# Wider products for q and k, and a first load order with held loads and eight products of zeros

## The chip, the cores and the metric

The kernel runs on one core of a Trainium2 chip. The metric is the device time of one execution in microseconds. The profile is of one such execution; its engines are TensorE (PE, with PEld for the loads of its stationary operand), VectorE (DVE), ScalarE (ACT), GpSimd (POOL) and SyncE (SP, which here issues every DMA).

## The reference

A decoder trunk of two layers over x of 256 x 1024 in float32. Each layer is a token mixer and a gated MLP with a causal convolution, each followed by `x <- LayerNorm(alpha * x + f(x))`.

```
# layer 0, mixer
u, v = split(gelu(x @ w_in))                 # 1024 -> 2 x 1024
v = layer_norm(v)
y = (u * (causal(w_s) @ v + b_s)) @ w_out    # 8 groups, chunks of 128 positions
# layer 1, mixer: 16 heads of 64, one block of 256 keys
q, k, v = split(x @ w_qkv); q = q * 64 ** -0.5
y = softmax(q @ k.T + bias_by_distance, causal) @ v @ w_o
# each layer
g, val = split(causal_conv3(x @ w_up))       # 1024 -> 2 x 2816
y = (gelu(g) * val) @ w_down
```

## The kernel before

The order of the work is made ahead of time, when the program is built. Every group of instructions is recorded as an operation with an engine, an estimated duration, what it reads and what it writes. `Plan.emit` then goes through all of them as a list scheduler: at each step the engine that can start earliest takes the ready operation that is due first, and the instructions are written out in the order of the planned starts. TensorE's main operations keep the order in which they were recorded, and operations marked `fill` go between them as soon as the plan holds them to be ready. Each engine's queue, SP's DMA queue among them, then runs strictly in that order. What an instruction really waits for on the chip is not taken from the plan: it follows from the memory that the instruction itself reads and writes.

All products are made from a high and a low part of float32 data (`whi`, `wlo` for weights, `xh`, `xl` for x, all float32r): hi·hi + hi·lo + lo·hi. Each 1 MB chunk of weights is loaded into one of two raw buffers (`raws`), ScalarE copies it into `whi` and VectorE subtracts that into `wlo` (`split`, L338 and L344). A chunk is prepared five chunks ahead (`prep`, `spent`); a raw buffer is free again when both parts are made. The chunks follow in one stream: a_v (4 chunks), a_u (4), a_out (4), f_up0, f_dn0, b_v, b_qk (8), b_o, f_up1, f_dn1.

At the start, the transposed x (`xT`) is loaded in four pieces into a scratch area `ff`, and the first two chunks of a_v in five. A `rank` (the numbers in `FIRST` and `XFIRST`) makes their due times; the scheduler otherwise picks as for any operation. `xT` is laid out by row tile t, then k, so a piece of one k has two runs of 128 columns in each partition. `gmlp` multiplies x with a_v in 16 steps (k, t), each of two halves of 512 columns with three products: first k = 0 to 3 for both row tiles, then k = 4 to 7 for t = 0, then for t = 1. Each half takes hi·hi, then hi·lo of the weights, then lo·hi. Then 8 groups of a_u follow (`cols_times`), with LayerNorm of v and the spatial products between them, and the output projection a_out.

In the second mixer, `moba`, `project(i, j)` makes q (j = 0) or k (j = 1) of head pair i with `cols_times`: for each of 8 k three products of 256 columns into the first half of a bank. ScalarE copies the first 128 columns in float32 (L338), and the high part (128 columns for q, 256 for k); VectorE subtracts the low part from the bank (L348). `scores(i - 1)` is recorded after `project(i, 1)`, then `turn(i - 2)`, and `apply(i - 3)` between the two projections; the last pairs follow inside the output projection. `bring` holds the loaded position bias of three head pairs. The up projection (`conv_up`) uses `cols_apart` instead: for each k one product of 512 columns with both parts of x as moving data and one of 256, and `joined` adds the two halves of the bank.

Of the kernel before, what the change touches and what calls it, by code (L numbers as in the profile page):

```python
# [45 lines left out]
T1_WAITS = (2600, 3300, 4000, 4700)  # L46
REST = 25000, 9000, 25000
AHEAD = 12000


class Buf:
# [25 lines left out]
class Plan:  # L77
# [44 lines left out]
    def emit(self):  # L122
        ops = self.ops
        for o in ops:
            for b in o.bufs:
                for q in b.prev:
                    o.deps.update(x for x in q.ops if x is not o)
            assert all(d.i < o.i for d in o.deps), "a group waits for one recorded after it"

        t = 0.0  # L130
        for o in ops:
            o.due = math.inf
            if o.eng == "pe":
                o.due = t
                t += o.ns
        for o in reversed(ops):
            if o.due == math.inf:
                o.due = t
            for d in o.deps:
                d.due = min(d.due, o.due - self.lag(d, o) - (d.ns + (2000.0 if d.eng == "sp" else 0.0)))  # L140
        for o in ops:
            if o.rank is not None:
                o.due = o.rank - 1e6

        succ, left = {}, {}
        for o in ops:
            left[o] = len(o.deps)
            for d in o.deps:
                succ.setdefault(d, []).append(o)
        engines = ("pe", "act", "dve", "pool", "sp")  # L150
        free = dict.fromkeys(engines, 0.0)
        cand = {e: [] for e in engines}
        bus, table = 0.0, None
        order = []
        bulk = [o for o in ops if o.eng == "pe" and not o.fill]
        nb = 0

        def ready(o):
            return max([0.0] + [d.end + self.lag(d, o) for d in o.deps])

        for o in ops:
            if not left[o]:
                cand[o.eng].append((0.0, o))
        while len(order) < len(ops):
            best = None
            for e in engines:
                c = cand[e]
                if e == "pe":
                    c = [x for x in c if x[1].fill or (nb < len(bulk) and x[1] is bulk[nb])]
                if not c:  # L170
                    continue
                s0 = min(max(free[e], r) for r, _ in c)
                now = [x for x in c if max(free[e], x[0]) <= s0 + 1.0]
                if e == "pe":
                    pick = min(now, key=lambda x: (not x[1].fill, x[1].due))
                else:
                    pick = min(now, key=lambda x: x[1].due)
                    for x in c:
                        s = max(free[e], x[0])
                        if x[1].due < pick[1].due and s0 < s < s0 + pick[1].ns and \  # L180
                                s + x[1].ns <= pick[1].due and x[1].due < s0 + pick[1].ns:
                            pick = x
                s = max(free[e], pick[0])
                if best is None or s < best[0]:
                    best = (s, e, pick)
            s, e, pick = best
            o = pick[1]
            cand[e].remove(pick)
            if o.eng == "pe" and not o.fill:
                nb += 1  # L190
            o.start = s
            if e == "sp":
                bus = max(bus, s + 1100.0) + o.nbytes / 360.0
                free[e] = max(s + 475.0, bus - 1500.0)
                o.end = bus
            else:
                extra = 0.0
                if o.table and o.table != table:
                    extra, table = 1300.0, o.table
                o.end = free[e] = s + o.ns + extra  # L200
            order.append(o)
            for x in succ.get(o, ()):
                left[x] -= 1
                if not left[x]:
                    cand[x.eng].append((ready(x), x))
        order.sort(key=lambda o: (o.start, o.i))
        for o in order:
            o.emit()
# [15 lines left out]
def trunk_kernel(ctx: ExitStack, tc: tile.TileContext, a: dict, out: bass.AP):  # L224
# [154 lines left out]
    chunks = {}  # L379


    FIRST = {0: [(0, 512, 0), (512, 1024, 2), (1024, 2048, 4)], 1: [(0, 1024, 6), (1024, 2048, 7)]}
    XFIRST = ((0, 1, 1), (1, 1, 3), (2, 2, 5), (4, 4, 8))

    def prep(i):
        name, c = stream[i]
        raw = raws.new()
        cuts = FIRST.get(i, [(0, CH, None)])
        for s, e, rank in cuts:
            load(raw.ap[:, s:e], a[name][c, :, s:e], [(raw, range(s // 256, e // 256))], rank=rank)  # L390
        subs = []
        for s in range(2):
            hi, lo = whi.new(), wlo.new()
            pieces = [(0, 512), (512, 1024)] if i in FIRST or i in FINE else [(0, SUB)]
            for b, e in pieces:
                src = raw.ap[:, s * SUB + b:s * SUB + e]
                split((hi, range(b // 256, e // 256), hi.ap[:, b:e]), (lo, range(b // 256, e // 256), lo.ap[:, b:e]),
                      (raw, range((s * SUB + b) // 256, (s * SUB + e) // 256), src))
            subs.append((hi, lo))
        chunks[i] = subs  # L400
# [25 lines left out]
    def xt_view(b):  # L426
        return b.ap

    xh, xl = xt_new()
    xT32 = place("ff", HALF, KT * S)  # L430
    xv32 = xT32.ap.rearrange("p (t k c) -> p t k c", t=NT, k=KT)

    def load_xt(k, n, rank):
        load(xv32[:, :, k:k + n, :], a["xT"][:, :, k:k + n, :], [(xT32, [(t, j) for t in range(NT) for j in range(k, k + n)])],
             rank=rank)
        for t in range(NT):
            parts = [(t, j) for j in range(k, k + n)]
            split((xh, parts, xt_view(xh)[:, t, k:k + n, :]), (xl, parts, xt_view(xl)[:, t, k:k + n, :]),
                  (xT32, parts, xv32[:, t, k:k + n, :]), by="dve" if k == 0 else "act")

    prep(0)
    for k, n, rank in XFIRST:
        load_xt(k, n, rank)
    for i in range(1, CHUNKS):
        prep(i)
    xtok = [Buf(t) for t in xs_]
    QUART = range(4)
# [193 lines left out]
    def gmlp():  # L641
        at = xt_at(xh, xl)
        pieces = [[(o, HALF, bank(True)) for o in (0, HALF)] for _ in range(NT)]
        order = [(k, t) for k in range(4) for t in range(NT)] + [(k, t) for t in range(NT) for k in range(4, KT)]
        v = []
        for k, t in order:
            rows_step(pieces[t], *at(k, t), *sub("a_v", k // 2, k % 2), k == 0, k == KT - 1)
            if t == NT - 1 and k % 2:
                spent("a_v", k // 2)
# [110 lines left out]
    def moba(h, l, scr):  # L760
        n4 = KT * S
        oh, ol = place("rr", 0, n4), place("rr", n4, n4)
        pring = Places("ff", [4 * P, 19 * S, 19 * S + P + S, 19 * S + 2 * (P + S)], P + S)
        qkring = [Places("ff", (j * 2 * P, j * 2 * P + P), P) for j in range(2)]
        qkparts = [[Ring(tiles(f"qk{n}{j}", 2, n, F32R)) for j in range(2)] for n in (P, S)]
        ering = Places("ff", [4 * S + x * (P + S) for x in range(6)], P + S)
        bring = Places("ff", [4 * S + 6 * (P + S) + x * 2 * S for x in range(3)], 2 * S)
        ohv, olv = (b.ap.rearrange("p (k s) -> p k s", k=KT) for b in (oh, ol))
        vb = rowring.new()
        vv = vb.ap.rearrange("p (t d) -> p t d", t=NT)  # L770
# [17 lines left out]

        def project(i, j):
            b, t = bank(), qkring[j].new()  # L790
            cols_times(b, h, l, *sub("b_qk", i, j))

            n, at2, scale = (P, P, DH ** -0.5) if j == 0 else (S, 0, 1.0)
            src, (th, tl) = b.ap[:, at2:at2 + n], (x.new() for x in qkparts[j])
            act(t.ap, b.ap[:, :P], AF.Copy, [b], [t], scale=scale, psum=True)
            act(th.ap, src, AF.Copy, [b], [th], scale=scale, psum=True)
            stt(tl.ap, src, scale, th.ap.bitcast(F32), ALU.mult, ALU.subtract, [b, th], [tl])
            t = (t, th, tl)
            held.setdefault(i, []).append(t)
            if j == 0:  # L800
                biases[i] = bring.new()
                load(biases[i].ap, bass.AP(tensor=scr.ap.tensor, offset=scr.ap.offset + 2 * i * DIST,
                                           ap=[[1, P], [DIST, 2], [1, S]]), [biases[i]], [scr])
            else:
                spent("b_qk", i)

        def scores(i):
# [4 lines left out]
            def both(o, seq):  # L812
                return [(bank2[hh].ap[:, o[0]:o[1]], x.ap[hh * DH:(hh + 1) * DH], y.ap[hh * DH:(hh + 1) * DH],
                         n == 0, n == len(seq) - 1) for n, (x, y) in enumerate(seq) for hh in range(2)]

            mms(both((0, P), [(q0, k0)]) + both((P, P + S), [(qh, kh), (qh, kl), (ql, kh)]),
                [q0, qh, ql, k0, kh, kl], bank2, fill=True)
            held[i] = [softmax(bank2[hh], bias, hh) for hh in range(2)]

# [81 lines left out]
def _layout(i):  # L901
# [10 lines left out]
    def paired(wa, wb):  # L912
# [3 lines left out]
    w_in, qkv = np.asarray(i["a_w_in"])[0], np.asarray(i["b_w_qkv"])[0]  # L916
    g = {
        "x": f(x.reshape(NT, P, D).transpose(1, 0, 2)),
        "xT": f(x.reshape(NT, P, KT, P).transpose(3, 0, 2, 1)),
        "a_v": by_rows(w_in[:, D:]),  # L920
        "a_u": f(tiles(w_in[:, :D]).reshape(4, 2, P, SUB).transpose(0, 2, 1, 3).reshape(4, P, CH)),
        "a_out": by_rows(np.asarray(i["a_w_out"])[0]),
# [45 lines left out]
```

## Time and profile before

| | |
|---|---|
| median of 3 runs | 573.56 us (572.23 to 574.41) |
| the profiled execution's own time | 573.82 us |
| its span, first to last instruction | 572.1 us |
| TensorE busy | 557.8 us (98%), 3226 products |
| VectorE busy | 459.9 us (80%) |
| ScalarE busy | 356.0 us (62%) |
| DMA | 110.93 MB, mean 194 GB/s |

The busy time of TensorE is modelled from pipelined products, so 98% does not say that it runs at its peak. The spacing of products in the timeline is the better measure of what one of them costs.

### The profile page before, as it was taken

The numbers are of one execution on the slowest core, as the hardware profiler recorded it, in microseconds if no ns is written. First come the engines' busy times: TensorE is split into PE (matmuls) and PEld (weight loads), VectorE is DVE, ScalarE is ACT, GpSimd is POOL, SyncE is SP. The second block draws the span as 40 slices with busy tenths as digits, with TensorE's granted clock in tenths as the row PEclk, the third lists the DMA queues.
The fourth block names the chain that finished last, engine by engine and source line by source line (L and its number), as shares of the span: only waits on it lengthen the run. The fifth ranks groups of instructions, "written<-read, shape, count | busy, mean of one in ns | idle before, by whom it ended". The sixth has DMA issues, their size and how long they took to land.

```text
span 572.1 us, 8555 instructions
## 1 busy us (share of the span) xinstructions
PE 557.8 (98%) x3226; PEld 482.7 (84%) x3226; DVE 459.9 (80%) x857; ACT 356.0 (62%) x652; POOL 11.5 (2%) x17
## 2 busy tenths in 40 slices
PE   6999999999999999999999999999999999999994
PEld 4799888888888878888899998788888888888884
DVE  4589989999999998467858767589989999997426
ACT  5474558776677786335569666367867767785300
POOL 0020010000000000001000000000000000000001
PEclk9999999999999999999999999999999999999998
DMA  7887644537554657652666542506456446566302
GB/s 259 307 300 288 257 147 158 211 147 255 187 220 149 221 224 263 227 212 92 221 221 236 207 156 84 222 1 211 158 215 226 183 186 214 196 245 231 144 1 73
DMA packets 20133, 110.93 MB, mean 194 GB/s; under 512 B 2251, under 2 KB 6268, under 8 KB 7676
## 3 DMA queue, kind: packets, MB, share of 16 engines
q1 hardware_dynamic: 20092, 110.39, 52.9%
q8 instruction: 25, 0.41, 0.3%
q14 instruction: 16, 0.13, 0.1%
HBM read 109.31 MB, written 1.07 MB: 193 GB/s over the span
## 4 chain that ended last, share of the span: by engine, by line
PE 91%; DMA 4%; DVE 2%; SPq 1%; ACT 0%; issue 0%; DVEq 0%
PE twos L326 52%; PE bank L326 38%; DMA raw<-in_a_v 2%; DMA raw<-in_a_u 2%; DVE wlo L344 1%; PE bank L332 1%; PE twos L332 1%; SPq L355 1%; ACT whi L338 0%; DVE x L348 0%; DVE ff L348 0%; DVE stat L494 0%; DVEq L964 0%; DVE stat L497 0%; DVE stat L499 0%
## 5 line engine op out<-in xcount | busy, mean ns | idle before, releaser
L344 DVE TENSOR_TENSOR wlo<-raw,whi 128x1024 fp32r<-128x1024 f32 (+1 forms) x212 | 228.9, 1103 | 39.2 <-ACT whi L338 38.6
L338 ACT ACTIVATE whi<-raw 128x1024 fp32r<-128x1024 f32 (+1 forms) x212 | 194.8, 954 | 58.7 <-DMA raw<-in_f_dn 24.5
L326 PE MATMUL twos<-xt,whi 128*128 128x512 f32 x640 | 222.2, 394 | 0.0
L326 PE MATMUL twos<-xt,wlo 128*128 128x256 f32 x640 | 177.3, 277 | 0.0
L326 PEld LDWEIGHTS twos<-xt,whi 128*128 128x128 f32 x640 | 120.0, 188 | 27.7
L326 PE MATMUL bank<-whi,rr 128*128 128x512 f32 x432 | 135.1, 391 | 0.0
L326 PEld LDWEIGHTS twos<-xt,wlo 128*128 128x128 f32 x640 | 120.2, 188 | 0.1
L326 PEld LDWEIGHTS bank<-whi,rr 128*128 128x128 f32 x432 | 81.1, 188 | 17.8 <-issue 1.0
L326 PE MATMUL bank<-wlo,rr 128*128 128x512 f32 x216 | 84.1, 389 | 0.0
L326 PE MATMUL bank<-xt,whi 128*128 128x256 f32 x384 | 71.8, 288 | 0.0
L348 DVE SCALAR_TENSOR_TENSOR ff<-ff,convc 128x254 f32<-128x254 f32 (+1 forms) x160 | 69.7, 478 | 0.5 <-ACT ff L338 0.2
L326 PEld LDWEIGHTS bank<-xt,whi 128*128 128x128 f32 x384 | 59.6, 191 | 2.0 <-issue 1.0
L338 ACT ACTIVATE ff<-twos 128x512 f32<-128x512 f32 (+1 forms) x56 | 31.0, 567 | 46.3 <-PE twos L326 43.9
L326 PE MATMUL bank<-xt,wlo 128*128 128x256 f32 x192 | 54.2, 282 | 0.0
L326 PEld LDWEIGHTS bank<-wlo,rr 128*128 128x128 f32 x216 | 40.6, 188 | 8.2
L338 ACT ACTIVATE ff<-ff,convc 128x256 f32<-128x256 f32 x80 | 45.6, 592 | 1.9 <-DVE ff L344 1.4
L326 PE MATMUL twos<-whi,xt 128*128 128x512 f32 x128 | 42.0, 396 | 0.0
L344 DVE TENSOR_TENSOR ff<-twos,ff 128x512 f32<-128x512 f32 (+1 forms) x48 | 30.9, 645 | 13.2 <-ACT ff L338 12.3
L338 ACT ACTIVATE ff<-bank,lncol 128x128 f32<-128x128 f32 x48 | 18.8, 458 | 30.5 <-PE bank L332 30.5
L326 PEld LDWEIGHTS bank<-xt,wlo 128*128 128x128 f32 x192 | 36.7, 191 | 0.0
L348 DVE SCALAR_TENSOR_TENSOR x<-x,bank 128x512 f32<-128x512 f32 x16 | 11.0, 686 | 27.4 <-PE bank L326 27.4
L326 PEld LDWEIGHTS twos<-whi,xt 128*128 128x128 f32 x128 | 24.1, 188 | 4.7
(70 smaller groups left out, 480.4 us busy)
## 6 DMA issues: line engine op xcount, KB each, us to landing
raw<-in_f_up SPq DMA_DIRECT2D x44, 1024.0 KB, 4.8
raw<-in_f_dn SPq DMA_DIRECT2D x22, 1024.0 KB, 4.8
raw<-in_b_qk SPq DMA_DIRECT2D x8, 1024.0 KB, 4.8
lnrow<-in_lnrow SPq DMA_DIRECT2D x5, 1024.0 KB, 5.8
raw<-in_a_u SPq DMA_DIRECT2D x4, 1024.0 KB, 4.7
raw<-in_a_out SPq DMA_DIRECT2D x4, 1024.0 KB, 5.1
raw<-in_b_v SPq DMA_DIRECT2D x4, 1024.0 KB, 4.8
raw<-in_b_o SPq DMA_DIRECT2D x4, 1024.0 KB, 4.8
```

What stands on the lines that cost most here:

```text
L326: nc.tensor.matmul(o, l, x, start=start, stop=stop)
L332: nc.tensor.transpose(o, x, ident.ap)
L338: plan.op("act", ns, lambda: nc.scalar.activation(o, x, func, **kw), r, w, table=table)
L344: dve(70 + 1.04 * flat(x), lambda: nc.vector.tensor_tensor(o, x, y, op=op), r, w)
L348: lambda: nc.vector.scalar_tensor_tensor(o, x, s, y, op0=op0, op1=op1), r, w)
L355: plan.op("sp", nbytes / 360.0, lambda: nc.sync.dma_start(o, src), r, w, nbytes=nbytes, rank=rank)
```

## The change

Start. Loads that have a rank are issued by SP strictly by it, before any other load. Ranks 5, 7, 9 and 10 have a small DMA ahead of them that copies 64 bytes from a part of an earlier load's buffer into a scratch tile (`hold`); the parts are those of ranks 0, 4, 6 and 7. Chunks 2 and 3 get ranks 9 and 10 and buffers of their own, in `ff` and in the row buffer of the LayerNorm weights, and are split in pieces of 512 columns. `xT` is laid out by k, then all 256 rows, so a piece is one run in each partition. The splits of x take two k at once. VectorE fills 512 columns with zeros, and eight products of them are recorded ahead of all others, into a bank that nobody reads. Step k = 0 of a_v runs for both row tiles together: high weights with the high part of x for both, then with the low part, then the low weights.

q and k. `project` uses `cols_apart`. ScalarE copies (scaled) the second half of the bank, VectorE adds the first half, ScalarE copies the high part and VectorE subtracts the low part, both now from SBUF. The buffers in `ff` move; `bring` has two places instead of three.

```diff
+WARM = 8
 # Plan.emit
+        ranked = sorted((o for o in ops if o.rank is not None), key=lambda o: -o.rank)
+                if e == "sp" and ranked:
+                    c = [x for x in c if x[1] is ranked[-1]]
+            if o.rank is not None:
+                ranked.remove(o)
 # trunk_kernel
-    FIRST = {0: [(0, 512, 0), (512, 1024, 2), (1024, 2048, 4)], 1: [(0, 1024, 6), (1024, 2048, 7)]}
+    FIRST = {0: [(0, 512, 0), (512, 1024, 2), (1024, 2048, 4)], 1: [(0, 1024, 6), (1024, 2048, 7)],
+             2: [(0, 2048, 9)], 3: [(0, 2048, 10)]}
     XFIRST = ((0, 1, 1), (1, 1, 3), (2, 2, 5), (4, 4, 8))
+    EARLY = {2: lambda: place("ff", HALF + KT * S, CH), 3: rowring.new}
+    HOLD = {5: (0, 0), 7: (0, SUB), 9: (1, 0), 10: (1, SUB)}
+    scratch = sb.tile([1, 16 * len(HOLD)], F32, name="scratch")
+    loaded, gates = {}, []
+    def hold(rank):
+        i, at = HOLD[rank]
+        g = Buf(scratch[:, 16 * len(gates):16 * len(gates) + 16])
+        load(g.ap, loaded[i].ap[:1, at:at + 16], [g], [(loaded[i], [at // 256])], nbytes=64, rank=rank - 0.5)
+        gates.append(g)
     def prep(i):
-        raw = raws.new()
+        raw = loaded[i] = EARLY.get(i, raws.new)()
         for s, e, rank in cuts:
-            load(raw.ap[:, s:e], a[name][c, :, s:e], [(raw, range(s // 256, e // 256))], rank=rank)
+            if rank in HOLD:
+                hold(rank)
+            load(raw.ap[:, s:e], a[name][c, :, s:e], [(raw, range(s // 256, e // 256))],
+                 gates[-1:] if i <= CHUNKS else (), rank=rank)
     def load_xt(k, n, rank):
+        if rank in HOLD:
+            hold(rank)
+        load(xT32.ap[:, sl], a["xT"][:, sl], [(xT32, parts)], gates[-1:], rank=rank)
+        for j in range(k, k + n, 2):
...
+            split((xh, parts, hv), (xl, parts, lv), (xT32, parts, xv), by="dve" if k == 0 else "act")
+    zeros, idle = place("rr", 0, HALF), bank()
+    dve(480, lambda: nc.vector.memset(zeros.ap.bitcast(F32), 0.0), (), [zeros])
+    for _ in range(WARM):
+        mms([(idle.ap, zeros.ap[:, :P], zeros.ap, True, True)], [zeros], [idle], fill=True)
 # gmlp
+        def first_step():
+            (hi, lo), x = sub("a_v", 0, 0), [at(0, t) for t in range(NT)]
+            for p in range(2):
+                for part, w in ((0, hi), (1, hi), (0, lo)):
+                    for t in range(NT):
+                        o, n, b = pieces[t][p]
+                        mms([(b.ap, x[t][part], w.ap[:, o:o + n], part == 0 and w is hi, False)],
+                            x[t][2][part:part + 1] + [(w, range(o // 256, (o + n) // 256))], [b])
+            plan.tick()
 # moba
-        pring = Places("ff", [4 * P, 19 * S, 19 * S + P + S, 19 * S + 2 * (P + S)], P + S)
-        qkring = [Places("ff", (j * 2 * P, j * 2 * P + P), P) for j in range(2)]
+        pring = Places("ff", [17 * S + x * (P + S) for x in range(4)], P + S)
+        qkring = [Places("ff", (j * 2 * S, j * 2 * S + S), S) for j in range(2)]
+        sring = Places("ff", [23 * S], S)
-        bring = Places("ff", [4 * S + 6 * (P + S) + x * 2 * S for x in range(3)], 2 * S)
+        bring = Places("ff", [4 * S + 6 * (P + S) + x * 2 * S for x in range(2)], 2 * S)
         def project(i, j):
-            cols_times(b, h, l, *sub("b_qk", i, j))
+            cols_apart(b, 0, h, l, *sub("b_qk", i, j))
-            src, (th, tl) = b.ap[:, at2:at2 + n], (x.new() for x in qkparts[j])
-            act(t.ap, b.ap[:, :P], AF.Copy, [b], [t], scale=scale, psum=True)
-            act(th.ap, src, AF.Copy, [b], [th], scale=scale, psum=True)
-            stt(tl.ap, src, scale, th.ap.bitcast(F32), ALU.mult, ALU.subtract, [b, th], [tl])
+            (th, tl), c = (x.new() for x in qkparts[j]), sring.new()
+            act(c.ap, b.ap[:, S:], AF.Copy, [b], [c], scale=scale, psum=True)
+            stt(t.ap, b.ap[:, :S], scale, c.ap, ALU.mult, ALU.add, [b, c], [t])
+            split((th, [0], th.ap), (tl, [0], tl.ap), (t, [0], t.ap[:, at2:at2 + n]))
 # _layout
-        "xT": f(x.reshape(NT, P, KT, P).transpose(3, 0, 2, 1)),
+        "xT": f(x.reshape(NT, P, KT, P).transpose(3, 2, 0, 1).reshape(P, KT * S)),
```

## Rows read from the trace of the kernel before

**Rows 1.** The page's fourth part: the chain of work that ended last, as shares of the span by engine.
```profile
PE 91%; DMA 4%; DVE 2%; SPq 1%; ACT 0%; issue 0%; DVEq 0%
```

**Rows 2.** Busy time by stretch (us from the span's start): the stretch and its length, then busy us and instructions of PE, PEld, DVE, ACT and POOL, the granted clock of TensorE (1.00 is full), the DMA engines' share and GB/s.
```profile
5.00:15.00 10.00, 9.92 (x30) 7.60 (x31) 6.72 (x14) 5.91 (x13) 0.00 (x0) 1.00 0.95 329
15.00:30.00 15.00, 13.66 (x59) 10.64 (x58) 6.78 (x8) 7.46 (x10) 0.00 (x0) 1.00 0.84 312
30.00:60.00 30.00, 29.77 (x238) 28.89 (x237) 29.04 (x48) 18.26 (x30) 3.70 (x3) 1.00 0.82 303
291.00:364.00 73.00, 73.00 (x604) 65.58 (x604) 54.83 (x179) 54.04 (x149) 0.00 (x0) 1.00 0.49 177
```

**Rows 3.** Whom TensorE's products waited for in the whole span: us in total, times, the longest.
```profile
PE bank L326 <- DVE xt L361: 5.0, 1, 5.0
PE bank L326 <- DVE wlo L344: 1.3, 2, 0.8
PE twos L326 <- DVE ff L348: 0.2, 1, 0.2
```

**Rows 4.** Timeline of TensorE in the first stage: start us, busy us, engine, line, operation, the count of merged instructions. The row at 32.11 is the first product with a_u.
```profile
5.00 0.77 PE L326 MATMUL bank<-whi,xt 128*128 128x512 f32 x1 [5.00 <-DVE xt L361]
5.85 0.79 PE L326 MATMUL bank<-wlo,xt 128*128 128x512 f32 x1
...
7.29 0.63 PE L326 MATMUL bank<-wlo,xt 128*128 128x512 f32 x1
...
8.57 0.63 PE L326 MATMUL bank<-wlo,xt 128*128 128x512 f32 x1
...
11.13 0.54 PE L326 MATMUL bank<-wlo,xt 128*128 128x512 f32 x1
...
12.66 0.39 PE L326 MATMUL bank<-wlo,xt 128*128 128x512 f32 x1
...
13.35 0.39 PE L326 MATMUL bank<-wlo,xt 128*128 128x512 f32 x1
...
32.11 0.40 PE L326 MATMUL bank<-xt,whi 128*128 128x256 f32 x2
```

**Rows 5.** Timeline of SP's queue at the start: issue of xT's third piece, of chunk 1 in two pieces, of chunks 2 and 3.
```profile
3.80 0.55 SPq L355 DMA_DIRECT2D ff<-in_xT  x1
4.40 1.07 SPq L355 DMA_DIRECT2D raw<-in_a_v  x2
...
10.93 4.51 SPq L355 DMA_DIRECT2D raw<-in_a_v  x2
```

**Rows 6.** Timeline of ScalarE: its first copy out of each newly landed load, and in brackets the idle time before it and what ended it.
```profile
4.29 0.63 ACT L338 ACTIVATE whi<-raw 128x512 fp32r<-128x512 f32 x1 [2.21 <-DMA raw<-in_a_v]
...
8.94 1.15 ACT L338 ACTIVATE whi<-raw 128x512 fp32r<-128x512 f32 x2 [0.97 <-DMA raw<-in_a_v]
...
11.85 2.42 ACT L338 ACTIVATE whi<-raw 128x512 fp32r<-128x512 f32 x4 [0.57 <-DMA raw<-in_a_v]
...
17.84 2.01 ACT L338 ACTIVATE whi<-raw 128x1024 fp32r<-128x1024 f32 x2 [2.27 <-DMA raw<-in_a_v]
21.67 2.01 ACT L338 ACTIVATE whi<-raw 128x1024 fp32r<-128x1024 f32 x2 [1.83 <-DMA raw<-in_a_v]
...
29.00 2.01 ACT L338 ACTIVATE whi<-raw 128x1024 fp32r<-128x1024 f32 x2 [2.21 <-DMA raw<-in_a_u]
```

**Rows 7.** DMA issues of the whole span: destination and source, count, KB of each, median us from issue to landing.
```profile
out<-x SPq DMA_DIRECT2D x8, 128.0 KB, 1.9
raw<-in_a_v SPq DMA_DIRECT2D x2, 256.0 KB, 3.5
...
lncol<-in_lncol SPq DMA_DIRECT2D x1, 24.0 KB, 6.4
```

**Rows 8.** Timeline of TensorE: two rows of the q and k stage, seven steps of three products apart, and two of the first up projection, eight steps of two products apart.
```profile
322.98 0.40 PE L326 MATMUL bank<-xt,whi 128*128 128x256 f32 x2
...
325.49 0.40 PE L326 MATMUL bank<-xt,whi 128*128 128x256 f32 x2
...
141.92 0.39 PE L326 MATMUL twos<-xt,whi 128*128 128x512 f32 x1
...
144.69 0.39 PE L326 MATMUL twos<-xt,whi 128*128 128x512 f32 x1
```

**Rows 9.** Timeline at the end of the q and k stage: the last pair's high and low part of k, its scores, and the low part of its attention output.
```profile
353.43 0.38 ACT L338 ACTIVATE qk<-bank 128x256 fp32r<-128x256 f32 x1 [0.56 <-PE bank L326]
...
354.01 0.42 DVE L348 SCALAR_TENSOR_TENSOR qk<-bank,qk 128x256 fp32r<-128x256 f32 x1
...
355.55 0.61 PE L326 MATMUL twos<-qk,qk 64*128 64x256 f32 x6
...
364.22 0.42 DVE L344 TENSOR_TENSOR rr<-twos,rr 128x256 fp32r<-128x256 f32 x1
```

**Rows 10.** The position bias: the last maximum of pair 0 on VectorE and the bias load issued behind it (timeline), a line of the chain by time that holds pair 2's scores (start us, us, count), and the bias loads of the whole span with their median landing.
```profile
301.37 0.29 DVE L827 CUSTOM_DVE_ANT_0 ff<-twos,ff 128x128 f32<-128x128 f32 x1
...
301.69 0.38 SPq L355 DMA_DIRECT2D ff<-rbscr  x1
...
313.45 0.78 PE twos L326 x10
...
ff<-rbscr SPq DMA_DIRECT2D x8, 256.0 KB, 4.3
```

More of the change, by code (lines that the diff above doesn't have):

```diff
@@ L430, in trunk_kernel, with cut @@
     xT32 = place("ff", HALF, KT * S)
-    xv32 = xT32.ap.rearrange("p (t k c) -> p t k c", t=NT, k=KT)
     def load_xt(k, n, rank):
[L434 to L439, printed above, removed]
-    prep(0)
-    for k, n, rank in XFIRST:
-        load_xt(k, n, rank)
-    for i in range(1, CHUNKS):
+        def cut(j, m):
+            return slice(j * S, (j + m) * S), [(t, i) for t in range(NT) for i in range(j, j + m)]
+        sl, parts = cut(k, n)
+        if rank in HOLD:
+            hold(rank)
+        load(xT32.ap[:, sl], a["xT"][:, sl], [(xT32, parts)], gates[-1:], rank=rank)
+        for j in range(k, k + n, 2):
+            m = min(2, k + n - j)
+            sl, parts = cut(j, m)
+            hv, lv = (both[:, j:j + m, o:o + S] for o in (0, S))
+            xv = xT32.ap[:, sl].rearrange("p (k x) -> p k x", k=m)
+            split((xh, parts, hv), (xl, parts, lv), (xT32, parts, xv), by="dve" if k == 0 else "act")
[3 more added lines that the diff above has]
+        mms([(idle.ap, zeros.ap[:, :P], zeros.ap, True, True)], [zeros], [idle], fill=True)
+    prep(0)
+    for x in XFIRST[:3]:
+        load_xt(*x)
+    prep(1)
+    load_xt(*XFIRST[3])
+    for i in range(2, CHUNKS):
         prep(i)
@@ L645, in gmlp @@
         v = []
+        def first_step():
[7 more added lines that the diff above has]
+            plan.tick()
         for k, t in order:
+            if k == 0:
+                if t == 0:
+                    first_step()
+                continue
             rows_step(pieces[t], *at(k, t), *sub("a_v", k // 2, k % 2), k == 0, k == KT - 1)
@@ L814, in both @@
                          n == 0, n == len(seq) - 1) for n, (x, y) in enumerate(seq) for hh in range(2)]
-            mms(both((0, P), [(q0, k0)]) + both((P, P + S), [(qh, kh), (qh, kl), (ql, kh)]),
+            q0_, k0_ = (type(t)(t.ap[:, :P]) for t in (q0, k0))
+            mms(both((0, P), [(q0_, k0_)]) + both((P, P + S), [(qh, kh), (qh, kl), (ql, kh)]),
                 [q0, qh, ql, k0, kh, kl], bank2, fill=True)
```

## The prediction

> **What bounds the kernel now.** I read the page first. The chain that ended last lies 91% on TensorE [rows 1], so what counts is where TensorE stands still or runs slowly, and how many products it must run. Next I read whom it waits for: over the whole run it lists 5.0 us before the first product, 1.3 us for low halves of weights, and 0.2 us later [rows 3]. From 41 us to the last product it has work without a gap. A microsecond won before 41 us therefore reaches the end, if nothing after it was hidden behind it; so does a microsecond of product time won in the q and k stage, where TensorE is busy for all of its 73 us [rows 2].
>
> The timeline of the first stage shows more than the list of waits. The v projection is 8 x 2 x 2 x 3 = 96 products of 512 columns. At the spacing of 12.66 to 13.35, three products in 0.68 us, they would take 96 x 0.2275 = 21.8 us; from 5.00 to the first a_u product at 32.11 they took 27.1 us [rows 4]. So 5.3 us are lost after the start, in three places:
> - Clock: from 7.29 to 8.57 three products take 1.28 us, 0.427 each, the 1.2 GHz level; from 12.66 on 0.2275, the 2.4 GHz level [rows 4]. The column of the granted clock reads 1.00 in these stretches [rows 2], so I go by spacing. Thirteen products start before 11.13: 13 x (0.427 - 0.2275) = 2.6 us.
> - Order: those thirteen took 6.13 us, not 13 x 0.427 = 5.55. The second product needs the low half of the first weights, and waits from 5.43 to 5.85: 0.6 us in all.
> - Data: the other 83 took 32.11 - 11.13 = 20.98 us, not 18.9: 2.1 us, at the third and fourth weight chunks.
>
> The data comes late because there are two raw buffers: chunk 2 is issued at 10.93, chunk 3 some 4 us later [rows 5]; ScalarE gets them at 17.84 and 21.67, and the first a_u chunk at 29.00 [rows 6].
>
> **Parts, start.** *Products of zeros.* The memset, some 0.2 to 0.7 us on an idle VectorE, lets them begin near 1.6. Eight at 0.427 us end at 5.0, just when the first data is there; at worst they push it by 0.1. Before, the clock rose 6.1 us after the first product (5.00 to 11.13); the busy stretch now begins 3.4 us earlier, so I put the rise at 7.8. Bounds: risen by 5.0, or at 11.1 as before. At 7.8, 6.5 products run at the low level instead of 13: **-1.3 us** (bounds -2.6 and 0).
>
> *Order of step k = 0.* Both row tiles take the high half before any takes the low half, so four to six products hide the 0.7 us of the split: **-0.6 us** (bounds 0 and -0.6).
>
> *Loads.* The 64-byte loads write a scratch that nothing reads, while each reads a buffer that an earlier load fills. So SP stops at it until that earlier load has landed, and what is issued next need not wait for the 64 bytes themselves. Behind the stopped load stands all of SP's queue. Gate by gate: the first waits for part 0, which is there at 4.29 [rows 6], and SP is free for it near 3.8, where xT's third piece is issued now [rows 5]: half a microsecond. The second waits for the last part of chunk 0, there at 8.9 before [rows 6]; with x in runs twice as long I take 8.2. The first half of chunk 1 is queued by then, so the DMA engines still have 768 KB. The second half of chunk 1 is then issued near 8.8 and lands near 12.3 (a load of 256 KB took 3.5 us from issue to landing [rows 7]). The gate of chunk 2 opens when the first half of chunk 1 is there (11.85 before [rows 6], 11.0 now): issued at 11.5, landed behind 1 MB of others at 16. The gate of chunk 3 opens at 12.3; it lands at 18.6. Against 17.84 and 21.67 that is 2 and 3 us sooner, since these two now have memory of their own, and a_u's first chunk, next in the first raw buffer, follows near 21 instead of 29. TensorE, with the rise at 7.8, finishes k = 0 at 9.1, waits 0.5 for the low half of k = 1 and 0.3 at k = 2, reaches chunk 2 at 17.9 (high half there at 16.6, low at 17.4, now split in pieces of 512) and chunk 3 at 20.6 (19.2, 19.9). Of 2.1 us some 0.75 stay: **-1.35 us** (bounds 0 and -2.1).
>
> Start together: **-3.2 us**, the v stage ends near 28.9. Who could give it back? VectorE is busy 29.0 of the 30 us from 30 to 60, but idle for 3.3 us of 5 to 15 and 8.2 us of 15 to 30 [rows 2]: with a_u's first two chunks landing 8 us sooner, their 4.7 us of low halves move into that idle time, more than the 3.2 us by which the stage moves up.
>
> The Trainium skill, "DMA: Bandwidth & Descriptors", section "Anatomy of one DMA", says that DMA engines do not wait on semaphores, the issuing sequencer does, and that a small transfer still costs about 2 us; by it a chain of four gates, if each had to land, would add some 8 us of DMA silence (an estimate from that page). The shortest landing here, 1.9 us for a store, agrees with the second half, and a 24 KB load behind large ones took 6.4 [rows 7].
>
> **Parts, q and k.** Each of 16 halves has 8 steps of three 256-column products, now one of 512 and one of 256: the columns are the same, 128 products fewer. From 322.98 to 325.49 seven steps of three take 2.51 us, 0.359 each; the up projection already has the pair, and eight take 2.77 us, 0.346 [rows 8]. 128 x 0.013 = **-1.7 us** (1.4 to 2.0 by the rounding of these rows; 0 in a rival below). The Trainium skill, "TensorE: Matmul & The Clock Gate", section "Back-to-back issue gap", gives a product about 2.5 ns beyond its columns; by that the saving would be 0.3 us. The rows give 13 ns, and I go by them.
>
> The price: evacuation is now copy, add, copy, subtract, four steps over two engines, instead of copy and subtract. VectorE gets about 16 x 0.42 = 6.7 us more [rows 9], on 54.8 of 73 us; ScalarE less than that on 54.0 [rows 2]: hidden. What is late next is scores, by about two operations, 0.8 us. Within the stage the next projection covers it. At the end there is less cover: the last pair's low half ends at 364.6 [rows 9], and by the count of products in the output projection it is wanted near 365.3. I take 0 and bound it by 1 us. The bias ring of two instead of three makes load i wait for the maximum of pair i - 2: the third buffer's successor went out at 301.69, right behind the maximum of pair 0 [rows 10]; pair 2's load would go there now, it lands some 4.3 us later, and its scores run at 313.45 [rows 10]: hidden. The rest of the layout change moves buffers only: 0, hidden by the same projections; 1 us at most if one of them is wanted early.
>
> **Sum.** -1.3 - 0.6 - 1.35 - 1.7 = -4.9 us. Against the profiled execution's own 573.82 (span 572.1 and 1.7 around it) that is **568.9**; the median before, 573.56, lies 0.3 lower. 0.5% is 2.9 us, about what a measurement of this kernel tells from no change; faster means below 570.7.
>
> **Rivals.**
> - *The gates hold the loads too long* (the other side: slower). If every held load leaves only after the 64 bytes landed behind all that is queued, each gate drains the queue and then costs about 2 us in which nothing moves (1.9 us for the shortest landing, 6.4 for a small one in the queue [rows 7]). Chunk 1's second half then lands near 16, chunk 2 near 22, chunk 3 near 26.7, and the v stage ends near 36.5: 4.4 us later than now, with q and k still -1.7: 576.5. It decides from chunk 3 landing later than about 23. For it: the plan itself counts such a wait. Against it: no other instruction takes the scratch as an operand. 0.10.
> - *The clock does not rise earlier*, zeros or not: the 1.3 us go, and a slower first stage waits less for data: the v stage ends near 30.5, -1.6 - 1.7: 570.5. For it: nothing here ran zeros. 0.13.
> - *The start is given back* on VectorE between 30 and 60, where it has 1 us of idle time [rows 2]: only q and k remain, about 572.1. For it: 97% busy; against it: 11 us of idle time before. 0.12.
> - *q and k save nothing*, because a product costs only its columns or because scores come late at the end: -3.2: 570.6. Against it: the measured pair [rows 8]. 0.07.
> - The forecast, 0.58, with its own range 567.0 to 570.4.
>
> Faster takes the forecast and about half of the second and fourth cases, on the edge of the bound: 0.70. Within 0.5%: the third, the other halves: 0.21. Slower: the first, 0.09. The range for 8 in 10 runs from the clock risen by 5.0 and data that keep up (about 2 us under the forecast) to just beyond the start given back: 566.8 to 572.5.
>
> **What would show it.** Eight products before 5.0, and the spacing of 0.2275 from about 7.8; no gap after the first real product; chunk 2 with ScalarE near 16, chunk 3 near 18.6, a_u's first chunk near 21; the first a_u product near 28.9; TensorE without waits from there to the end; the q and k steps at 0.346, the stage about 1.7 us shorter. The prediction is wrong if SP stands at a gate while the DMA engines are silent, if the spacing stays at 0.427 until 11, if TensorE waits for VectorE between 30 and 60, or if scores or the last pair hold it after 350.

## The result: slower, and the profile after

The changed kernel takes 577.97 us (median of 6 runs, 575.26 to 579.66) against 573.49 for the kernel before: ratio 1.0088, 95% interval [1.0067, 1.0109]. The forecast was 568.9. The profiled execution took 576.64, its span is 574.9 (572.1 before).

The list of whom TensorE waited for, whole span (us in total, times, the longest), answers to [rows 3]:

```profile
PE bank L338 <- ACT ff L344: 2.1, 4, 0.6
PE bank L332 <- DVE nhalf L445: 1.5, 1, 1.5
PE bank L332 <- ACT whi L344: 0.9, 1, 0.9
PE twos L332 <- ACT xt L344: 0.9, 1, 0.9
PE bank L332 <- DVE wlo L350: 0.4, 2, 0.2
```

Before, all that counted was in the first 41 us. Now there are five waits for ScalarE, 3.0 us together, at tiles of the LayerNorm's way back into columns (`ff`, `xt`). The chain that ended last shows ScalarE too, 2% where [rows 1] have 0%:

```profile
PE 91%; DMA 5%; ACT 2%; DVE 1%; issue 1%; SPq 0%; DVEq 0%
```

Where the 2.8 us between the two profiled executions lie, from the starts of TensorE's products at the edges of each stretch (in the up projections and at the end of q and k, those with the low weights):

| stretch | before | after | change |
|---|---|---|---|
| start to first a_u product | 32.11 | 30.04 | -2.07 |
| to the up projection, first layer (with the first passage through LayerNorm) | 62.78 | 64.01 | +1.23 |
| first up projection, its 320 steps | 111.05 | 113.15 | +2.10 |
| to the products of q and k (second passage) | 84.77 | 86.00 | +1.23 |
| q and k | 62.34 | 61.36 | -0.98 |
| to the second up projection (third passage) | 40.02 | 41.50 | +1.48 |
| to the last product, and from it to the end of the span | 179.03 | 178.84 | -0.2 |

The start and the q and k stage won 3.05 us. Three passages lost 3.94, and the first up projection, of which the diff touches nothing, lost 2.10.

Start, TensorE's timeline, against [rows 4] (zeros, first real products, the wait at the third chunk, the first a_u product):

```profile
1.51 3.78 PE L332 MATMUL bank<-rr 128*128 128x512 f32 x8 [1.51 <-DVE nhalf L445]
5.09 1.68 PE L332 MATMUL bank<-whi,xt 128*128 128x512 f32 x4
6.61 0.62 PE L332 MATMUL bank<-wlo,xt 128*128 128x512 f32 x2
7.07 1.17 PE L332 MATMUL bank<-whi,xt 128*128 128x512 f32 x4
...
18.49 0.51 PE L332 MATMUL bank<-whi,xt 128*128 128x512 f32 x1 [0.92 <-ACT whi L344]
...
30.04 0.40 PE L332 MATMUL bank<-xt,whi 128*128 128x256 f32 x2
```

Four products take 1.52 us from 5.09, the next two 0.46: the spacing falls from the 1.2 GHz level to 0.23, the 2.4 GHz level, shortly after 6 us. Before, that was at 11.

ScalarE's first copies from chunk 1 in its two parts, from chunks 2 and 3 and from the first a_u chunk, against [rows 6]; and SP's queue around the gates, against [rows 5]:

```profile
10.21 1.16 ACT L344 ACTIVATE whi<-raw 128x512 fp32r<-128x512 f32 x2 [0.60 <-DMA raw<-in_a_v]
12.93 1.16 ACT L344 ACTIVATE whi<-raw 128x512 fp32r<-128x512 f32 x2 [1.56 <-DMA raw<-in_a_v]
...
17.81 2.19 ACT L344 ACTIVATE whi<-ff 128x512 fp32r<-128x512 f32 x4 [2.50 <-DMA ff<-in_a_v]
20.28 2.20 ACT L344 ACTIVATE whi<-lnrow 128x512 fp32r<-128x512 f32 x4 [0.28 <-DMA lnrow<-in_a_v]
22.97 1.06 ACT L344 ACTIVATE whi<-raw 128x1024 fp32r<-128x1024 f32 x1 [0.49 <-DMA raw<-in_a_u]
```
```profile
10.27 0.51 SPq L361 DMA_DIRECT2D scratch<-raw  x1
10.82 0.58 SPq L361 DMA_DIRECT2D ff<-in_a_v  x1
12.92 0.50 SPq L361 DMA_DIRECT2D scratch<-raw  x1
13.47 0.58 SPq L361 DMA_DIRECT2D lnrow<-in_a_v  x1
```

A gate is issued once the part that it reads has landed, and the load behind it 0.55 us later; nobody waits for the 64 bytes. Chunk 2 is with ScalarE as late as before (17.81, 17.84), chunk 3 1.4 us and a_u's first chunk 6 us sooner.

The first passage, TensorE's timeline, first of before, then of after:

```profile
85.77 0.60 PE L332 MATMUL bank<-ident,x 128*128 128x128 f32 x4
86.12 0.48 PE L326 MATMUL twos<-whi,xt 128*128 128x512 f32 x1
86.44 0.39 PE L326 MATMUL twos<-wlo,xt 128*128 128x512 f32 x1
86.67 0.40 PE L326 MATMUL twos<-whi,xt 128*128 128x512 f32 x1
86.91 0.60 PE L332 MATMUL bank<-ident,x 128*128 128x128 f32 x4
```
```profile
85.55 1.04 PE L338 MATMUL bank<-ident,x 128*128 128x128 f32 x8
87.10 0.44 PE L338 MATMUL bank<-ident,ff 128*128 128x128 f32 x2 [0.51 <-ACT ff L344]
88.10 0.44 PE L338 MATMUL bank<-ident,ff 128*128 128x128 f32 x2 [0.57 <-ACT ff L344]
88.29 0.48 PE L332 MATMUL twos<-whi,xt 128*128 128x512 f32 x1
```

Before, transposes and products of the up projection take turns, and ScalarE works behind the products. After, twelve transposes stand in a row, and TensorE waits for ScalarE twice. The diff edits none of these instructions; their written order has changed. The same pair of waits is back near 389 us, and one of 0.89 at 278.

The first up projection, eight steps apart, against 141.92 and 144.69 of [rows 8] (2.77 us):

```profile
150.07 0.40 PE L332 MATMUL twos<-xt,whi 128*128 128x512 f32 x1
...
152.90 0.40 PE L332 MATMUL twos<-xt,whi 128*128 128x512 f32 x1
```

Now 2.83 us. By the full resolution of the starts a pair takes 0.3533 us where it took 0.3467, evenly over the whole stage; the second up projection runs at 0.3467 in both.

### The profile page after: what moved, and what is told of

The parts are those of the page before. It is cut to its first block, busy times and chain, and to the rows that moved or that the text cites. A ratio compares the mean times of both kernels' runs of the same rounds, so it can differ in the third digit from the quotient of the medians.

```text
span 574.9 us, 8307 instructions
## 1 busy us (share of the span) xinstructions
PE 561.4 (98%) x3106; PEld 477.7 (83%) x3106; DVE 464.2 (81%) x874; ACT 361.0 (63%) x654; POOL 10.2 (2%) x17
## 4 chain that ended last, share of the span: by engine, by line
PE 91%; DMA 5%; ACT 2%; DVE 1%; issue 1%; SPq 0%; DVEq 0%
PE twos L332 52%; PE bank L332 37%; DMA raw<-in_a_u 3%; DMA raw<-in_a_v 2%; PE twos L338 1%; PE bank L338 1%; ACT ff L344 1%; ACT whi L344 1%; DVE wlo L350 1%; DVE x L354 0%; SPq L361 0%; ACT ff L803 0%; ACT xt L344 0%; DVE ff L354 0%; DVE stat L532 0%
## 5 line engine op out<-in xcount | busy, mean ns | idle before, releaser
L350 DVE TENSOR_TENSOR wlo<-raw,whi 128x1024 fp32r<-128x1024 f32 (+1 forms) x208 | 224.7, 1096 | 41.9 <-ACT whi L344 41.7
L344 ACT ACTIVATE whi<-raw 128x1024 fp32r<-128x1024 f32 (+1 forms) x208 | 191.6, 957 | 58.5 <-PE bank L332 31.4
L332 PE MATMUL twos<-xt,wlo 128*128 128x256 f32 x640 | 179.5, 280 | 0.0
L332 PE MATMUL bank<-xt,whi 128*128 128x256 f32 (+1 forms) x256 | 71.0, 347 | 0.0
L354 DVE SCALAR_TENSOR_TENSOR ff<-ff,convc 128x254 f32<-128x254 f32 (+1 forms) x160 | 67.4, 478 | 1.2 <-ACT ff L344 1.2
L344 ACT ACTIVATE ff<-ff,convc 128x256 f32<-128x256 f32 x80 | 44.0, 594 | 14.5 <-DVE ff L350 14.4
L332 PEld LDWEIGHTS bank<-xt,whi 128*128 128x128 f32 x256 | 44.0, 190 | 6.8 <-issue 1.0
L332 PE MATMUL twos<-whi,xt 128*128 128x512 f32 x128 | 40.8, 392 | 0.9 <-ACT xt L344 0.9
```

The source lines that it names most:

```text
L332: nc.tensor.matmul(o, l, x, start=start, stop=stop)
L344: plan.op("act", ns, lambda: nc.scalar.activation(o, x, func, **kw), r, w, table=table)
L350: dve(70 + 1.04 * flat(x), lambda: nc.vector.tensor_tensor(o, x, y, op=op), r, w)
L354: lambda: nc.vector.scalar_tensor_tensor(o, x, s, y, op0=op0, op1=op1), r, w)
```

## The experiments

Two questions: who makes the waits in the passages, and what makes the pair slower. The first has an offline clue. Going through the written plan of each kernel, one finds stretches in which the plan itself leaves TensorE idle:

```
planned TensorE idle after 30 us (us from start: us idle)
before, only q and k      none
after, only the start     87: 0.78  88: 0.77  88.5: 0.37 | 264: 0.10 0.10  266: 1.40 | 375: 0.78  376: 0.77
```

In the plan a gate is a load that must land before the next one is issued, about 2 us for each; four gates move the planned start by 8 us. The list scheduler then meets all later choices at other times.

### One part of the change at a time, and the gates

`a_start` has all hunks of the start and leaves `project` of q and k as before; `a_qk` has the hunks of `moba` alone. In `a_unplanned` the gates stay in SP's queue, but the loads behind them don't name them, so the plan counts no wait:

```diff
-                 gates[-1:] if i <= CHUNKS else (), rank=rank)
+                 (), rank=rank)
...
-        load(xT32.ap[:, sl], a["xT"][:, sl], [(xT32, parts)], gates[-1:], rank=rank)
+        load(xT32.ap[:, sl], a["xT"][:, sl], [(xT32, parts)], rank=rank)
```

`a_nohold` has no gates: `HOLD = {}`.

> Only the start of the change; q and k as before. Theory 1 (the planner): the gates count in the plan as loads that must land, the plan therefore runs up to 12 us behind the chip at the start, and its order at the three passages from a LayerNorm to the next projection leaves TensorE waiting there, 1.1, 1.2 and 1.4 us in the profile of the changed kernel. Then the v stage ends near 30.0, 2.1 us sooner than before, the three waits stand as in the changed kernel, and the time is 573.5 - 2.1 + 3.7 = 575.1 (up to 2.1 more if the steps of an up projection take 0.353 instead of 0.347 again). Rival (q and k): the passages are disturbed by the new q and k evacuation. Then the waits are not here and the time is about 571.4.

> Only the change of q and k; the start as before. Theory 1: the plan up to the q and k stage is that of the kernel before, so none of the three waits, and the stage alone counts: steps at 0.346 give 573.5 - 1.7 = 571.8, steps at 0.353, as seen in the changed kernel, 573.5 - 0.8 = 572.7. Rival (q and k cost): the longer evacuation or the smaller bias ring makes TensorE wait for scores: at or above 573.5, with waits between 291 and 364 us.

> The changed kernel, whose plan no longer lets the loads wait for the gates (they take no gate among what they read); the gates still stand in SP's queue at the same ranks, so the chip waits at the same places. Theory 1: the plan is closer to the chip, the waits at the first and the third passage go, one of about 0.9 us stays at the second, and the time is 573.5 - 2.1 - 1.0 + 1.0 = 571.4 (up to 2.1 more with slow steps in an up projection, 0.8 less with fast ones in q and k). Rival (the chip): an earlier start leaves VectorE and ScalarE with a backlog at the first passage whatever the order is; then the waits stay at 3.7 us and the time at 575 or more.

> The changed kernel without the four gates; the strict order of the ranks, the buffers of their own for chunks 2 and 3, the zeros and the q and k part stay. Theory 1: as without the gates in the plan, 571.4 and no wait at the first and third passage. What the gates do on the chip: if they keep large loads from taking the bandwidth of small ones, the first half of chunk 0 and the pieces of x come later here and TensorE waits more before 10 us; if the queue runs in order anyway, chunk 2 is with ScalarE at 17.8 or sooner and the v stage ends at 30.0 or sooner.

Measured, beside 572.15 us for the kernel before on the same chip:

| run | us | ratio, 95% interval | first a_u product | pair in the two up projections |
|---|---|---|---|---|
| a_start | 577.76 | 1.0096 [1.0065, 1.0126] | 31.31 | 0.3533, 0.3467 |
| a_qk | 571.55 | 0.9995 [0.9979, 1.0012] | as before | 0.3467, 0.3467 |
| a_unplanned | 571.50 | 0.9987 [0.9970, 1.0005] | 31.69 | 0.3467, 0.3467 |
| a_nohold | 570.18 | 0.9962 [0.9943, 0.9981] | 28.84 | 0.3467, 0.3467 |

The start alone makes the loss. In its list of waits the passages stand as in the changed kernel; with the same gates in the queue but out of the plan they are gone, but for 0.3 us in the second:

```profile
PE bank L338 <- ACT ff L344: 2.1, 4, 0.6
...
PE twos L332 <- ACT xt L344: 0.9, 1, 0.9
```
```profile
PE bank L332 <- ACT whi L344: 2.0, 1, 2.0
PE bank L332 <- DVE nhalf L445: 1.5, 1, 1.5
PE bank L332 <- DVE wlo L350: 0.7, 3, 0.2
PE twos L332 <- DVE xt L350: 0.3, 1, 0.3
```

(The first fence is of `a_start`, the second of `a_unplanned`.) On the chip gates are no gain either: without them the three late chunks are with ScalarE at 16.22, 18.70 and 21.20 (17.81, 20.28, 22.97 with them), and the first a_u product is the earliest of all. Over all profiled executions, chunk 2 is with ScalarE at 16.2 to 17.5 in the three kernels without gates (`b_ten` and `b_cold`, below, are the others) and at 17.8 to 19.5 in the four executions with all four; the first a_u product comes at 28.8 to 30.4 and at 30.0 to 31.7, which overlap. `a_nohold` beats both kernels.

### The planner alone

`c_late` is the kernel before with one number of the planner changed, and no instruction more or less:

```diff
-        bus, table = 0.0, None
+        bus, table = 8000.0, None
```

> The kernel before, with not one instruction added or taken away: only the planner is told that the load bus is taken until 8 us, as if the first loads landed that much later, so that its list of instructions comes out in another order. The plan then holds the same waits of TensorE as that of the changed kernel: 0.78, 0.77 and 0.43 us in the first passage, 1.40 in the second, 0.78 and 0.77 in the third. Theory 1 (the planner's order alone makes the passages' waits): TensorE waits for ScalarE near 87, 277 and 390 us, 3.7 us together, the first product with a_u near 32.1 as before, 572.5 + 3.7 = 576.2 us, and 2.1 us more for each up projection that falls into the slower spacing: 576 to 580. Theory 2 (the gates or the other loads on the chip make the waits, the plan only mirrors them): no wait in the passages, 572.5 us.

Measured: 578.83 us beside 572.24 for the kernel before, ratio 1.0106 [1.0083, 1.0129], first a_u product at 31.96. Its list of waits (the first line is the wait for the first data, as in [rows 3]):

```profile
PE bank L326 <- DVE xt L361: 5.0, 1, 5.0
PE bank L332 <- ACT ff L338: 2.2, 4, 0.6
PE bank L326 <- DVE wlo L344: 1.5, 2, 0.8
PE twos L326 <- ACT xt L338: 0.9, 1, 0.9
...
```

The same five waits for ScalarE stand at the same places, and both up projections run at 0.3533. No gate, no zeros, no new load order, no wider product: the written order alone costs as much as the whole change did. That settles the passages. All traces agree with it: from the last product of the first mixer's output projection to the first of the 320 steps TensorE takes 13.87 to 13.89 us in the four profiled executions with these waits (the changed kernel twice, `a_start`, `c_late`) and 12.45 in the eight others, and the third passage takes 41.4 to 41.5 us against 39.9 to 40.1. Which of the scheduler's choices tips over is not settled; by the plan, one or two gates leave the passages without idle time, three give 2.4 us, four 5.1.

### Two gates, and the zeros

`b_two` keeps the gates ahead of the third and fourth chunk: `HOLD = {9: (1, 0), 10: (1, SUB)}`. `b_ten` and `b_cold` have no gates and `WARM = 10` and `WARM = 0`; both have plans without idle time in the passages.

> The changed kernel with two of its four gates, those ahead of the third and the fourth chunk of a_v. The plan holds no wait in the three passages with two gates (four give 5.0 us, three 2.4 us). Theory 1 (the passages' waits come from the planner, which counts a gate's landing as waited for): no TensorE wait over 0.2 us in the passages near 87, 277 and 389 us, and the first up projection at 0.3467 us for a pair of products; the start pays for two gates on the chip: a_u between 28.84 (none) and 31.69 (four, unplanned), say 30.0, and a total of 570.2 - 0.4 + 1.2 = 571.0 us. Rival A (any gate in the plan brings the passages' waits): about 574. Rival B (gates help where they stand ahead of half megabytes, by leaving the queues to the small loads): a_u at 28.8 or before, 569.8 or less.

> The changed kernel without any gate, and with ten products of zeros instead of eight. Without gates the plan still holds one wait of 0.85 us of TensorE in the passage before the products of q and k, and the run without gates (570.18 us) shows 0.38 us there; with ten products of zeros the plan comes out without that wait. Theory 1 (a wait that the plan holds is paid on the chip, and nothing else differs): 570.2 - 0.4 = 569.8 us, no idle stretch of TensorE between 250 and 290 us, the first product with a_u still at 28.8. Rival (the passage is paid elsewhere, as the softmaxes set the pace of the stage of q and k): 570.2, with the products of q and k starting earlier and the second up projection not. If the pair of products in the first up projection falls into its slower spacing (0.3533 instead of 0.3467 us), 2.1 us come on top of either.

> The changed kernel without any gate and without the eight products of zeros; order and place of the first loads as there. Theory 1 (the zeros are worth what the prediction said, 1.3 us, since the clock then rises behind real products): first product with a_u at 30.1 instead of 28.84; the plan has no wait in the passages here, which gives back 0.4: 570.2 + 1.3 - 0.4 = 571.1 us. Rival (the loads and their splitting set the start, and the zeros only fill a wait): a_u at 28.9, 569.8 us. In between: the first chunks' products are slower but the wait for the third chunk takes part of it, about 0.5 us left.

Measured, beside 572.62 us:

| run | us | ratio, 95% interval | first a_u product | pair in the two up projections |
|---|---|---|---|---|
| b_two | 576.57 | 1.0058 [1.0038, 1.0079] | 31.27 | 0.3533, 0.3533 |
| b_ten | 570.85 | 0.9975 [0.9962, 0.9988] | 30.39 | 0.3467, 0.3467 |
| b_cold | 570.67 | 0.9963 [0.9948, 0.9978] | 29.86 | 0.3467, 0.3467 |

`b_two` is as the first theory has it in the passages: no wait (its one wait behind 30 us is 0.9 us, at 39). The rest of that theory fails: the time is 5.6 us above its 571.0, and both its up projections run at the slow spacing, twice 2.1 us. Eight steps of the first take 2.83 us:

```profile
149.67 0.40 PE L332 MATMUL twos<-xt,whi 128*128 128x512 f32 x1
...
152.50 0.40 PE L332 MATMUL twos<-xt,whi 128*128 128x512 f32 x1
```

So the slow spacing does not need the passages' waits, and it is worth as much as they are.

`b_cold` shows what the zeros are worth. Its clock rises behind real products, late:

```profile
5.04 2.23 PE L332 MATMUL bank<-whi,xt 128*128 128x512 f32 x4 [5.04 <-ACT whi L344]
...
9.63 1.05 PE L332 MATMUL bank<-wlo,xt 128*128 128x512 f32 x2
10.49 0.63 PE L332 MATMUL bank<-whi,xt 128*128 128x512 f32 x1
...
11.23 0.63 PE L332 MATMUL bank<-whi,xt 128*128 128x512 f32 x2
11.69 0.40 PE L332 MATMUL bank<-wlo,xt 128*128 128x512 f32 x1
```

Two products take 0.86 us up to 10.49, the 1.2 GHz level, and two take 0.46 from 11.23, the 2.4 GHz level. Yet the first a_u product comes at 29.86, between the two runs with zeros (28.84, 30.39), and the time ratio equals that of `a_nohold`. Both figures fall between the two expectations: the first product nearer to the theory that prices the zeros (30.1), the time, by its ratio, nearer to the rival. The zeros are worth no more than what these runs differ by among themselves: the first a_u products of the two runs with zeros lie 1.55 us apart. That difference comes from the loads: ScalarE's copy of chunk 0's last part starts at 8.32 and 10.04 in the two runs with zeros, from the same queue of loads. In `b_cold` TensorE, slower at first, waits for nothing behind its first product; in `a_nohold` it waits 0.6 us in the first stage, in `b_ten` 1.8. `b_ten` was to be 0.4 us faster than `a_nohold` for its plan without idle time; its later start hides that, and the run is inconclusive.

### The two spacings

`b_again` is the changed kernel once more. `c_marks` is `b_two` with the first product of a sum run again ahead of itself, at five places of each up projection:

```diff
+AGAIN = {5: (512,), 8: (256,), 11: (128,), 14: (512, 512), 17: (512, 512, 512)}
...
+            for n in twice:
+                o, l, x = seq[0][:3]
+                nc.tensor.matmul(o[:, :n], l, x[:, :n], start=True, stop=True)
```

> The changed kernel itself once more, for the spacing of its products. Theory 1 (the slower spacing in the first up projection follows from the order of what TensorE does before it): 0.3533 us for a pair of products there again, and 0.3467 in the second, with the time near 577.9. Theory 2 (which of the two spacings a stage falls into differs from execution to execution): the first stage can be at 0.3467, with 575.8, or the second at 0.3533, with 580.

> The kernel with two gates (first and second up projection both at 0.3533 us for a pair of products), in which, at five places of each up projection, the first product of a sum is run again ahead of itself and overwritten: once with 512 columns, once with 256, once with 128, then twice and three times with 512; eight extra products of some 1.4 us in each stage, the order and all else as before. Theory 1 (a spacing is a state that TensorE's stream carries on from product to product, set by the entrance into the stage): an extra product shifts the stream against itself and at one or more of the five places the spacing goes from 0.3533 to 0.3467 us and stays there to the next mark. Theory 2 (the spacing is set by what stands around the stage in this kernel: where its tiles lie, what the other engines do): 0.3533 us between all the marks of the stage.

`b_again`: 576.32 us in its one execution, with the stages exchanged: the first up projection at 0.3467, the second at 0.3533. Eight steps of each:

```profile
149.79 0.39 PE L332 MATMUL twos<-xt,whi 128*128 128x512 f32 x1
...
152.56 0.39 PE L332 MATMUL twos<-xt,whi 128*128 128x512 f32 x1
```
```profile
449.66 0.40 PE L332 MATMUL twos<-xt,whi 128*128 128x512 f32 x1
...
452.49 0.40 PE L332 MATMUL twos<-xt,whi 128*128 128x512 f32 x1
```

2.77 us, then 2.83. The same program in the same order (the two traces list the same 3106 products one after the other): so the order does not fix which spacing a stage gets, and my first theory of this run falls. Whether both executions ran on the same chip is not recorded.

`c_marks`: 578.33 us, also one execution. Around its second mark, eight steps before it, the extra product of 256 columns, eight steps after it:

```profile
125.32 0.40 PE L336 MATMUL twos<-xt,whi 128*128 128x512 f32 x1
...
128.14 0.40 PE L336 MATMUL twos<-xt,whi 128*128 128x512 f32 x1
...
128.50 0.28 PE L334 MATMUL twos<-xt,whi 128*128 128x256 f32 x1
...
128.97 0.39 PE L336 MATMUL twos<-xt,whi 128*128 128x512 f32 x1
...
131.75 0.39 PE L336 MATMUL twos<-xt,whi 128*128 128x512 f32 x1
```

2.82 us before, 2.78 after (0.3533 and 0.3467 by the full resolution). The five marks do: once 512, stays at 0.3533; 256, falls to 0.3467; 128, back to 0.3533; twice 512, 0.3467; three times 512, 0.3533. In the second up projection the five do exactly the same. Each spacing holds until the next mark. So the spacing is a state that TensorE's stream of products carries along, set by what came just ahead; neither the places of tiles nor the work of other engines has to change for it. What in TensorE keeps the two patterns, and what chooses at the entrance, is open. A link to the plan there is: of the twelve up projections profiled in kernels whose plan waits for two gates or more or has the late bus, nine entered at 0.3533; of the twelve in the other kernels, before among them, none.

## Why the prediction was wrong

**The step that failed** is the sentence that a microsecond won before 41 us reaches the end "if nothing after it was hidden behind it". I asked who could give the time back on the chip, VectorE between 30 and 60, and it did not: up to the output projection the two microseconds were still there. I did not ask what the edit does to the order of everything behind it, though that order is computed from the very estimates that the gates enter. In the first rival I even noted that the plan counts a gate's landing as a wait, and used it only as evidence on the gates. The passages cost 3.94 us, and the slow spacing, which came with the new plans, 2.1 us for each stage that falls into it. The profiled execution has one such stage and lies 1.3 us below the median; how many the others had is not recorded.

**Zeros and clock, -1.3.** Eight products from 1.51, the first real one at 5.09: as predicted. The rise came between 6.0 and 6.4 and not at 7.8, better than forecast. Worth: nothing that could be told from the scatter of the start (`b_cold`), since TensorE with the early clock waits 1.1 us for the third chunk (the rows at 18.49 and the low half behind it). I summed a clock term and a data term for one stage, where only the one that ends last counts.

**Order of step k = 0, -0.6.** The wait for the low half of the first weights is gone; what follows runs into the loads as well.

**Loads, -1.35.** The gates work as I read them, and rival one's price of a wait for the 64 bytes did not come; the gates land some 4 us after issue, with nobody waiting:

```profile
scratch<-raw SPq DMA_DIRECT2D x4, 0.1 KB, 3.9
```

The Trainium skill, "DMA: Bandwidth & Descriptors", section "Anatomy of one DMA", gives about 2 us as the fixed cost of a DMA on the path from GpSimd. The prediction's estimate from it, some 8 us of silence if four gates must each land, does not come true in this trace: a gate took 3.9 us to land, issued by SP among larger loads, but the load behind it did not wait for that.

But chunk 2 came at 17.8 instead of 16, and TensorE waited 0.9 for it; chunk 3 came at 20.3 instead of 18.6. Chunk 2 was issued at 10.82, sooner than the 11.5 of the prediction, and took 7.0 us to land where the prediction had 4.5. The start gave 2.07 of the 3.2 us here, 1.8 in `b_again` and 0.8 in `a_start`, whose start is the same. Without gates chunks 2 and 3 come at 16.2 and 18.7 in `a_nohold` and the start gives 3.3, but 1.7 and 2.3 in `b_ten` and `b_cold`: the term was too large by what the gates hold back and by what the landings of the first loads differ from execution to execution.

**q and k, -1.7.** It gave 0.98 here, 0.79 in `a_qk` (61.55 us from first to last product, 62.34 before). The term took 0.346 for a pair from a stage in the fast spacing. In this stage the stream is broken off often by scores and outputs, and between two breaks it runs at either spacing: the mean of the steps without a break is 0.351 to 0.352 in all nine traces with the wide product, and 0.359 before. 128 x (0.359 - 0.3515) = 1.0 us is the term by that. Evacuation, bias ring and the last pair cost nothing, as predicted: no wait in the list stands there.

**Rivals.** The slower side was right only in sign: its 576.5 lies beside the 576.64 of the profiled execution by luck, since no load waited for the 64 bytes and chunk 3 did not come after 23. "The start is given back on VectorE" did not occur. "q and k save nothing" is what the total of `a_qk` cannot tell from the truth.

## What to carry to other kernels

When the instruction order comes from a planner, an edit that changes a planned duration or adds a planned wait can reorder every later stage. So compare the written order of the stages that the diff does not touch, and give the planner the wait that the chip will have, not the dependency that was convenient to write. Two gains at one place are not a sum: whichever of clock and data ends last counts.

## What the runs showed of the hardware

- A pair of products of 512 and 256 columns repeats in one of two patterns, 0.3533 or 0.3467 us, for 300 steps without a change; one extra product of 128 or 256 columns switched it, in both up projections of one execution. Two executions of one program can have them in different stages. That is 2.1 us, 0.4% of this kernel, for nothing that any wait shows.
- Eight products of zeros from 1.51 brought TensorE's clock to the 2.4 GHz level by 6.4 us; without them, with real products from 5.04, it was there by 11.2; the column of the granted clock reads 1.00 from 5 to 15 us either way.
